# A bidirectional state-space layer's scan chains joined in pairs, its phasor tables packed, and new instruction durations in the list scheduler

## The chip, the cores and the metric

The kernel runs on one core of a Trainium2 chip. The metric is the device time of one execution in microseconds. The profile comes from one execution that the hardware profiler recorded. TensorE (PE) multiplies matrices, VectorE (DVE), ScalarE (ACT) and GpSimd (POOL) work on elements, and SyncE (SP) issues the transfers.

## What is computed

One layer of a hybrid encoder over 2048 positions and 1024 channels. A modulated RMS norm and one input projection feed three groups of heads; their outputs are joined, projected, normed and added to the input; a gated MLP with a depthwise convolution of width 3 follows.

```python
h = rms_norm(x, g_pre_mix[l]) * (1.0 + sc_m) + sh_m
u, f, q, k, v = jnp.split(h @ w_in[l], splits, axis=-1)
y_ssm = s5_mixer(u, ...)         # 24 groups x 16 channels, 64 complex states, two directions
y_fft = fourier_mixer(f, w_fft[l])       # 2-D DFT over positions and channels
y_att = window_attention(q, k, v, sink[l])       # +-128 positions, 6 query heads
y = concatenate([y_ssm, y_fft, y_att]) @ w_out[l]
x = x + gt_m * rms_norm(y, g_post_mix[l])
# then: norm, w_up, convolution, gelu(gate) * val, w_down, norm, gated residual add
```

The part that matters here is `s5_mixer`: for each group and each direction a linear recurrence h[t] = a h[t-1] + b u[t] with a complex diagonal a runs along the positions (backwards for the second direction), and y is read from both directions' states.

## The kernel before

**How the recurrence is tiled.** Eight positions are folded into one step, so that a group's input `U` is a 128x256 tile (8 positions x 16 channels, by 256 steps). A group has 64 states, each with a real and an imaginary part, so its states fill 128 partitions; two directions of 256 steps make a row of 512. VectorE's scan instruction knows no complex numbers. The kernel therefore turns the states by a phase so that each scan has a real factor: a row of 256 steps is split into 16 blocks of 16, table `t1c`/`t1s` holds the cosine and sine of the phase at each place of a block, and `t2c`/`t2s` those at the 16 block ends. The tables are tiles of 16x48: place first, then the 48 pairs of group and direction.

**One chain** (`s5_chain`, L953 on) handles one group. TensorE makes the two projections XA and XB in PSUM. VectorE multiplies each by a table (`gg`, `tt_`), adds them, and scans 512 elements. The block ends (2 directions x 16) then go through nine small instructions of 32 or 30 elements, with two products by a permutation matrix on TensorE between them (it swaps real and imaginary halves), and one of the nine is a scan over the 16 block ends. The result is added to the first place of each block, the 512 elements are scanned again, and two more products by `t1s` and `t1c` lead to the closing matrix products, a copy and a store. The two calls that read the tables are

```python
tsel = lambda tab: tab[:, :, s0:s0 + 2].rearrange("p b d -> p d b")
ta = yield from self.tt(ta, v4(gg), v4(XA), bt(tsel(self.t1c)), M)
```

so that the table's innermost step is 48 elements (L968, L980).

**Pairs.** `s5_pair` (L861 on) prepares two groups at once: projection matrices on POOL (on VectorE for the first two pairs), transposed by TensorE; output matrices on POOL; a small matrix `M0` by eight transfers. It puts two entries in a queue, one for each group. Three workers (`N_CH`) take entries from it. There are 12 pairs, 24 groups, and room for three pairs in preparation.

**What sets the order.** The whole kernel is written as processes that yield the engine, a duration and the time from which their inputs are there. A list scheduler (`Sched.run`) always emits the instruction that can start earliest by these numbers, and among equals the one of the higher rank; each engine then runs its instructions in the emitted order. Chains rank before the input projections, Fourier heads and output parts, which fill the gaps. Durations stand in the helpers: `tt` (L275, a tensor_tensor), `ts` (L280, a tensor_scalar), `scan` (L300). Every matmul is issued at L318, every activation at L272, every transfer at L267. PSUM is shared by tags: four banks `s` for the chains and, later, attention; three `z`; one `m`.

**What follows.** The gated unit of the state-space heads, the attention (16 blocks of 128 positions, two workers), Fourier products and the rest of the input projection share the time after the scans; then come the output projection, the norms and the MLP.

Of the kernel before, what the change touches and what calls it, by code (L numbers as in the profile page):

```python
# [16 lines left out]
P = 128  # L17
# [26 lines left out]
S5_MUL = "V"  # L44
# [29 lines left out]
N_CH = 3  # L74
# [128 lines left out]
class Builder:  # L203
# [71 lines left out]
    def tt(self, t, out, a, b, op, eng="V"):  # L275
        t = yield (eng, 0.07 + (0.00105 if eng == "V" else 0.0022) * cols(out), t)
        (self.V if eng == "V" else self.G).tensor_tensor(out, a, b, op)  # L277
# [22 lines left out]
    def scan(self, t, out, d0, d1):  # L300
        t = yield ("V", 0.1 + 0.00105 * cols(out), t)
        self.V.tensor_tensor_scan(out, d0, d1, 0.0, ALU.mult, ALU.add)  # L302
        return t + self.LAT
# [114 lines left out]
    def setup(self):  # L418
# [8 lines left out]
        self.par, self.sgn = self.const([P, 3, 48]), self.const([P, 1])  # L427
# [302 lines left out]
    def s5_consts(self):  # L730
# [98 lines left out]
        for f in ends:  # L829
            t = max(t, (yield ("w", f)))  # L830
# [4 lines left out]
        self.t1c, self.t1s, self.t2c, self.t2s = tabs  # L835
# [25 lines left out]
    def s5_pair(self, b, t, slots):  # L861
# [44 lines left out]
        left = [2, 0.0]  # L906
# [46 lines left out]
    def s5_chain(self):  # L953
        PE = self.PE
        v4 = lambda a: a.rearrange("p (d a b) -> p d a b", d=2, a=16)
        v3 = lambda a: a.rearrange("p (d a) -> p d a", d=2)
        fl = lambda a: a.rearrange("p d a -> p (d a)")
        bt = lambda a: a.unsqueeze(2).to_broadcast([P, 2, 16, 16])
        M, ADD, SUB = ALU.mult, ALU.add, ALU.subtract
        while True:  # L960
            while not self.s5q:
                if self.s5n == 0:
                    return
                yield ("w", self.f_s5q)
            b, g, t, f_u, f_m, wt, U, RT, M0, Vf, Vs, left, slots = self.s5q.pop(0)
            t = max(t, (yield ("w", f_u)))
            s0 = 4 * b + 2 * g
            tsel = lambda tab: tab[:, :, s0:s0 + 2].rearrange("p b d -> p d b")  # L968
            tb_ = yield ("acq", self.bank["s"], 2)
            XA, XB = self.ps("s"), self.ps("s")  # L970
            rhs = (U[:, g, :], U[:, g, ::-1])
            ops = [(XX[:, d * 256:d * 256 + 256], wt[:, 2 * g + d, o:o + 128], rhs[d], True, True)
                   for XX, o in ((XA, 0), (XB, 64)) for d in range(2)]
            ta = yield from self.mm(max(t, tb_), ops[:2])
            tb = yield from self.mm(max(t, tb_), ops[2:])
            t12, rxs = self.u([2, 512]), self.u([768])
            gg, tt_ = t12[:, 0], t12[:, 1]
            rx, sc = rxs[:, 0:512], self.shape(rxs[:, 512:768], [8, 2, 16])
            tx = yield from self.act(t, v4(rx), bt(RT[:, 0, 2 * g:2 * g + 2]), AF.Copy)
            ta = yield from self.tt(ta, v4(gg), v4(XA), bt(tsel(self.t1c)), M)  # L980
            tb = yield from self.tt(tb, v4(tt_), v4(XB), bt(tsel(self.t1s)), M)
            self.free(tb, XB)
            t = yield from self.tt(max(ta, tb), gg, gg, tt_, ADD, eng=S5_ADD)
            t = yield from self.scan(max(t, tx), tt_, rx, gg)

            pe_ = XA
            ends = v4(tt_)[:, :, :, 15]
            c2, s2 = tsel(self.t2c), tsel(self.t2s)
            tc_ = yield from self.tt(t, sc[:, 1], ends, c2, M)
            t = yield from self.mm(t, [(pe_[:, 0:32], self.perm, ends, True, True)])  # L990
            t = yield from self.tt(t, sc[:, 0], v3(pe_[:, 0:32]), s2, M)
            t = yield from self.tt(t, sc[:, 1], sc[:, 1], sc[:, 0], ADD)
            t = yield from self.scan(t, fl(sc[:, 2]), fl(RT[:, 1, 2 * g:2 * g + 2]), fl(sc[:, 1]))
# [1120 lines left out]
```

## Time and profile before

| | us |
|---|---|
| median of three runs | 2199.02 (2198.71 to 2199.77) |
| the profiled execution's own time | 2203.73 |
| its span, first to last instruction | 2202.0 |
| TensorE busy | 2004.0 (91%) |
| VectorE busy | 1597.4 (73%) |
| ScalarE busy | 984.3 (45%) |
| POOL busy | 246.6 (11%) |
| mean granted TensorE clock | 0.955 of full speed |

A row of groups reads: line of the program, engine, operation, output <- inputs with shapes (u is a tile in SBUF, ps one in PSUM, c a constant, d a tensor in memory), number of instructions, then busy time in us and mean ns of one, then the engine's idle time just before them and what ended most of it. A row of stretches gives the stretch and its length, each engine's busy time with its instructions, the granted TensorE clock, the share of the transfer engines and GB/s. A row of waits gives who waited for whom, us in total, times and the longest. A row of the timeline gives the start, the length, the engine, the line and the instruction. A float32 matmul leaves two records.

### The profile page before, as it was taken

How to read it: one execution, taken by the hardware profiler on the slowest of the kernel's cores; microseconds unless marked ns; L12 is line 12 of the kernel's file. 1: busy time of each engine (PE TensorE's matmuls, PEld its weight loads, DVE VectorE, ACT ScalarE, POOL GpSimd, SP SyncE). 2: the span in 40 equal slices, each digit the busy share in tenths (PEclk: the TensorE clock that was granted, in tenths of full speed). 3: DMA queues.
4: the chain of work that ended last, by engine and by line, in shares of the span. 5: the costliest groups of instructions: out<-in, count | busy, mean ns of one | idle time of the engine just before them, and what ended most of it. 6: DMA issues, size and time to landing. Idle time of an engine off the chain costs nothing.

```text
span 2202.0 us, 27575 instructions
## 1 busy us (share of the span) xinstructions
PE 2004.0 (91%) x10120; PEld 1001.0 (45%) x10120; DVE 1597.4 (73%) x2400; ACT 984.3 (45%) x1670; POOL 246.6 (11%) x310
## 2 busy tenths in 40 slices
PE   6778787889998858898999999999999999999997
PEld 2335565445454425443444444444444444444445
DVE  8999999886676584879988885565656665446456
ACT  3623233336576556556655553444444433222321
POOL 0565545020100000000000000000000000011002
PEclk9988898999999979799999999999999999999998
DMA  9351123673735273335655557565656494538533
GB/s 367 105 190 60 41 93 135 210 267 124 241 118 173 95 244 103 114 127 210 244 205 186 187 187 300 195 220 203 219 201 224 144 343 143 182 119 292 188 110 110
DMA packets 206667, 397.31 MB, mean 180 GB/s; under 512 B 19522, under 2 KB 111939, under 8 KB 206531
## 3 DMA queue, kind: packets, MB, share of 16 engines
q1 hardware_dynamic: 206530, 395.55, 52.2%
q8 instruction: 79, 1.29, 0.2%
q14 instruction: 58, 0.47, 0.1%
HBM read 258.93 MB, written 134.98 MB: 179 GB/s over the span
## 4 chain that ended last, share of the span: by engine, by line
PE 61%; DVE 25%; ACT 5%; issue 4%; DMA 3%; POOL 1%; SPq 1%; DVEq 0%; POOLq 0%; ACTq 0%
PE ps L318 61%; DVE u L277 12%; DVE u L291 8%; ACT u L272 5%; DVE u L302 2%; DVE u L446 1%; DMA u<-d 1%; POOL u L277 1%; SPq L267 1%; DMA u<-w_up 1%; DMA d<-u 1%; DVE u L284 0%; DVE u L410 0%; DMA u<-x 0%; DVE u L1327 0%
## 5 line engine op out<-in xcount | busy, mean ns | idle before, releaser
L318 PE MATMUL ps<-u,u 128*128 128x512 f16 (+9 forms) x9306 | 1918.7, 366 | 123.5 <-DVE u L277 35.7
L318 PEld LDWEIGHTS <-u 128*128 128x128 f16 (+1 forms) x9334 | 872.2, 101 | 1041.1 <-issue 174.5
L277 DVE TENSOR_TENSOR u<-u,u 128x512 f32<-128x512 f32 (+10 forms) x596 | 512.0, 892 | 107.0 <-ACT u L272 90.0
L272 ACT ACTIVATE u<-u 128x1024 f16<-128x1024 f32 (+8 forms) x483 | 403.2, 868 | 364.3 <-DVE u L277 158.8
L272 ACT ACTIVATE u<-ps 128x512 f32<-128x512 f32 (+6 forms) x511 | 276.3, 556 | 471.3 <-PE ps L318 445.7
L291 DVE SCALAR_TENSOR_TENSOR u<-u,c,u 128x1023 f32<-128x1023 f32 (+5 forms) x248 | 291.0, 1197 | 60.9 <-ACT u L272 55.2
L291 DVE SCALAR_TENSOR_TENSOR u<-ps,u 128x512 f32<-128x512 f32 (+3 forms) x231 | 152.4, 666 | 242.7 <-PE ps L318 201.1
L291 DVE SCALAR_TENSOR_TENSOR u<-u,u 128x1024 f16<-128x1024 f32 (+7 forms) x225 | 240.8, 1093 | 59.2 <-ACT u L272 55.8
L277 POOL TENSOR_TENSOR u<-u,u 128x288 f32<-128x288 f32 (+9 forms) x169 | 188.2, 1129 | 628.2 <-DVE u L291 459.1
L272 ACT ACTIVATE u<-u,c 128x1023 f32<-128x1023 f32 (+2 forms) x104 | 120.1, 1158 | 142.1 <-DVE u L291 122.0
L307 POOL MEMSET u<- 128x1 f32 x88 | 8.7, 99 | 1139.4 <-PE ps L318 510.9
L272 ACT ACTIVATE u<-u,st 128x384 f32<-128x384 f32 (+3 forms) x192 | 108.8, 596 | 35.6 <-DVE st L284 20.1
L318 PEld LDWEIGHTS ps<-u,u 128*128 128x128 f32 (+1 forms) x532 | 95.9, 194 | 62.3 <-DVE u L277 33.9
L277 DVE TENSOR_TENSOR u<-u 128x512 f32<-128x512 f32 (+8 forms) x184 | 92.3, 513 | 23.6 <-ACT u L272 22.4
L318 PE MATMUL ps<-u,c 128*128 128x32 f32 (+4 forms) x190 | 67.9, 465 | 43.7 <-DVE u L302 19.3
L318 PE MATMUL ps<-c,u 128*128 128x128 f16 (+1 forms) x568 | 61.9, 231 | 17.9 <-ACT u L272 11.4
L272 ACT ACTIVATE c<-u 128x2 f32<-128x2 f32 (+1 forms) x88 | 17.9, 203 | 130.3 <-DVE u L291 130.1
L1327 DVE CUSTOM_DVE_ANT_0 u<-ps,u 128x384 f32<-128x384 f32 (+1 forms) x96 | 49.1, 537 | 30.0 <-PE ps L318 29.3
L302 DVE TENSOR_TENSOR_SCAN u<-u,u 128x512 f32<-128x512 f32 (+1 forms) x72 | 68.9, 964 | 1.1 <-ACT u L272 0.9
L318 PEld LDWEIGHTS ps<-u,c 128*128 128x128 f32 (+1 forms) x190 | 30.7, 185 | 77.2 <-DVE u L302 29.7
L291 DVE SCALAR_TENSOR_TENSOR u<-u,st,u 128x384 f16<-128x384 f32 (+1 forms) x96 | 55.7, 609 | 11.9 <-ACT u L272 11.6
L277 DVE TENSOR_TENSOR u<-ps,u 128x512 f32<-128x512 f32 (+2 forms) x96 | 56.0, 600 | 7.6 <-PE ps L318 6.9
(52 smaller groups left out, 367.2 us busy)
## 6 DMA issues: line engine op xcount, KB each, us to landing
u<-d SPq DMA_DIRECT2D x226, 512.0 KB
d<-u SPq DMA_DIRECT2D x158, 512.0 KB
d<-u SPq DMA_DIRECT2D x111, 256.0 KB
u<-w_ada SPq DMA_DIRECT2D x48, 512.0 KB
u<-w_up SPq DMA_DIRECT2D x44, 512.0 KB
u<-d SPq DMA_DIRECT2D x66, 256.0 KB
u<-x SPq DMA_DIRECT2D x32, 512.0 KB
u<-d SPq DMA_DIRECT2D x24, 511.0 KB
```

The costliest lines, as they stand in the source:

```text
L267: self.SP.dma_start(out, in_)
L272: self.S.activation(out, in_, func, **kw)
L277: (self.V if eng == "V" else self.G).tensor_tensor(out, a, b, op)
L291: self.V.scalar_tensor_tensor(out, a, s, b, op0, op1)
L302: self.V.tensor_tensor_scan(out, d0, d1, 0.0, ALU.mult, ALU.add)
L307: (self.V if eng == "V" else self.G).memset(out, v)
L318: self.PE.matmul(o, a, b, start=st, stop=sp, skip_group_check=chain)
L446: V.tensor_tensor_reduce(out=w, in0=w, in1=self.crep, op0=ALU.mult, op1=ALU.add, scale=1.0, scalar=0.0, accum_out=mod[:, j:j + 1])
L1327: V.tensor_tensor_reduce(out=s_, in0=o, in1=self.bias[h // 2][:, h % 2, bo:bo + nk * 128], op0=ALU.add, op1=ALU.max, scale=1.0, scalar=-3e ...
```

## The change

1. The four tables are copied by ScalarE into tiles of 48x16 (the pair of group and direction first, the place innermost). The sign that VectorE put on the two sine tables is now a scale of the copy, from a new constant `nsg`.
2. One queue entry is a pair. A worker makes the opening part for both groups in turn (two PSUM banks each, freed after the products), then the small part once for both (60 or 64 elements), then the closing part for each. One further bank holds the block ends' products and both groups' results.
3. Two workers take the entries.
4. The durations of `tt` on both engines, `ts` on POOL and `scan` change.

```diff
-N_CH = 3
+N_CH = 2
...
     def tt(self, t, out, a, b, op, eng="V"):
-        t = yield (eng, 0.07 + (0.00105 if eng == "V" else 0.0022) * cols(out), t)
+        t = yield (eng, 0.155 + 0.00104 * cols(out) if eng == "V" else 0.4 + 0.0024 * cols(out), t)
...
     def ts(self, t, out, a, s1, s2, op0, op1=None, eng="V"):
-        t = yield (eng, 0.12 + (0.0008 if eng == "V" else 0.001) * cols(out), t)
+        t = yield (eng, 0.15 + (0.0008 if eng == "V" else 0.0018) * cols(out), t)
...
     def scan(self, t, out, d0, d1):
-        t = yield ("V", 0.1 + 0.00105 * cols(out), t)
+        t = yield ("V", 0.08 + 0.0023 * cols(out), t)
...
-        for ts_ in (t1s, t2s):
-            t = yield from self.ts(t, ts_, ts_, self.sgn, -1.0, M, M)
+        tn = yield from self.ts(0, self.nsg, self.sgn, -1.0, None, M)
+        byst = []
+        for f, (x, y) in zip(ends, ((t1c, t1s), (t2c, t2s))):
+            tf = yield ("w", f)
+            for src, sc in ((x, 1.0), (y, self.nsg)):
+                dst = self.u([48, 16])
+                t1 = yield from self.act(max(tf, tn), dst, src.rearrange("p j s -> p s j"), AF.Copy, scale=sc)
+                t = max(t, t1)
+                byst.append(dst)
...
-        for g in range(2):
-            self.s5q.append((b, g, max(tp, tr), f_u, f_m, wt, U, RT, M0, Vf, Vs, left, slots))
-            f, self.f_s5q = self.f_s5q, Fut()
-            f.set(0)
+        self.s5q.append((b, max(tp, tr), f_u, f_m, wt, U, RT, M0, Vf, Vs, slots))
+        f, self.f_s5q = self.f_s5q, Fut()
+        f.set(0)
...
+            gg, tt_, rx = (self.u([2, 512]) for _ in range(3))
+            sc = self.u([7, 4, 16])
+            tc, ts_, c2, s2 = (tab[:, 4 * b:4 * b + 4] for tab in (self.t1c, self.t1s, self.t2c, self.t2s))
+            for g in range(2):
+                ds = slice(2 * g, 2 * g + 2)
+                tb_ = yield ("acq", self.bank["s"], 2)
+                XA, XB = self.ps("s"), self.ps("s")
...
+                ta = yield from self.tt(ta, v4(gg[:, g]), v4(XA), bt(tc[:, ds]), M)
+                tb = yield from self.tt(tb, v4(tt_[:, g]), v4(XB), bt(ts_[:, ds]), M)
+                self.free(ta, XA)
+                self.free(tb, XB)
+                t = yield from self.tt(max(ta, tb), gg[:, g], gg[:, g], tt_[:, g], ADD, eng=S5_ADD)
+                t = yield from self.scan(max(t, tx), tt_[:, g], rx[:, g], gg[:, g])
+            tb_ = yield ("acq", self.bank["s"], 1)
+            pe_ = self.ps("s")
...
-            t = yield from self.mm(t, [(pe_[:, 0:32], self.perm, ends, True, True)])
+            t = yield from self.mm(t, [(pe_[:, 0:64], self.perm, ends, True, True)])
...
+            for g in range(2):
+                ds = slice(2 * g, 2 * g + 2)
+                t = yield from self.scan(tk, tt_[:, g], rx[:, g], gg[:, g])
+                t1 = yield from self.tt(t, v4(rx[:, g]), v4(tt_[:, g]), bt(ts_[:, ds]), M, eng=S5_MUL)
+                t = yield from self.tt(t, v4(gg[:, g]), v4(tt_[:, g]), bt(tc[:, ds]), M)
...
+                y = pe_[:, 256 * g:256 * g + 256]
```

The order in which the built programs' instructions stand shows the move. A scan is the row SCALAR_TENSOR_TENSOR of L302 there. VectorE before, in the small part of two chains that stand beside each other (u_1407 and u_1408 belong to one group, u_1448 and u_1449 to another; u_89 and u_90 are the tables of the block ends):

```order
L277 TENSOR_TENSOR u_1449<-u_1448,u_89 128x32
L307 MEMSET u_1370 128x8
L905 COPY u_1370<-c_82 128x4x15 x2
L277 TENSOR_TENSOR u_1372<-u_1372,ps_1506 16x2x16
L277 TENSOR_TENSOR u_1372<-u_1372 16x2x16
L277 TENSOR_TENSOR u_1408<-ps_1387,u_90 128x2x15
L277 TENSOR_TENSOR u_1449<-ps_1422,u_90 128x32
L277 TENSOR_TENSOR u_1408<-u_1408 128x2x15
L277 TENSOR_TENSOR u_1449<-u_1449 128x32
L277 TENSOR_TENSOR u_1408<-u_1408,c_82 128x2x15
```

VectorE now, at a like place (u_1376 and u_1379 belong to one pair, u_1265 to u_1267 to another; u_1063 and u_1078 are the packed tables of the places, u_1098 and u_1108 those of the block ends):

```order
L302 SCALAR_TENSOR_TENSOR u_1379<-u_1132,u_1379 128x64
L277 TENSOR_TENSOR u_1134<-u_1134,ps_1522 16x2x16
L277 TENSOR_TENSOR u_1379<-u_1379,u_1098 128x4x15
L277 TENSOR_TENSOR u_1134<-u_1134 16x2x16
L277 TENSOR_TENSOR u_1379<-ps_1487,u_1108 128x4x15
L277 TENSOR_TENSOR u_1267<-u_1266,u_1078 128x512
L277 TENSOR_TENSOR u_1379<-u_1379 128x4x15
L277 TENSOR_TENSOR u_1265<-u_1266,u_1063 128x512
L277 TENSOR_TENSOR u_1379<-u_1379,c_82 128x4x15
```

The small steps are twice as wide and come once for a pair, and a 512-wide product of the other pair stands between them where small steps of other groups stood.

TensorE before, late in the scans (c_79 is the permutation, ps_2820 a tile of the rest of the projections, u_2621 to u_2623 a pair's opening products):

```order
L318 MATMUL ps_2820<-u_194,u_590 128x512
L318 MATMUL ps_2638<-u_2657,c_79 128x32
L318 LDWEIGHTS u_590
L318 MATMUL ps_2820<-u_196,u_590 128x512
L318 MATMUL ps_2843<-u_2621,u_2623 128x256
L896 MATMUL ps_2764<-c_78,u_2671 128x128 x4
L318 MATMUL ps_2843<-u_2621,u_2623 128x256
L318 MATMUL ps_2844<-u_2621,u_2623 128x256 x2
```

TensorE now, a little past the middle of the scans (ps_2357 holds a closing pair's results, ps_2519 a tile of the projections):

```order
L318 MATMUL ps_2519<-u_659,u_1164 128x512
L318 MATMUL ps_2357<-u_2002,u_2003 128x256
L318 MATMUL ps_2357<-u_2255,u_2003 128x255 x2
L318 MATMUL ps_2357<-u_2257,u_2002 128x255 x2
L318 MATMUL ps_2496<-u_2408,c_79 128x64
L318 MATMUL ps_2551<-u_2272,u_84 16x128 x4
L318 LDWEIGHTS u_1164
L318 MATMUL ps_2519<-u_657,u_1164 128x512
```

A permutation now serves four rows of block ends, and tiles of 24 projection matmuls stand around the chains' steps from the middle of the scans on; ahead of the last permutation there stand 736 matmuls of 128x512, 476 before. From matmul 4103 before and 4112 now (of 9751 and 9727) TensorE's order is the same for 4452 matmuls.

More of the change, by code (lines that the diff above doesn't have):

```diff
@@ L964, in s5_chain @@
                 yield ("w", self.f_s5q)
[L965 to L973, printed above, removed]
@@ L982, in s5_chain @@
[L982 to L988, printed above, removed]
+            b, t, f_u, f_m, wt, U, RT, M0, Vf, Vs, slots = self.s5q.pop(0)
+            t0 = max(t, (yield ("w", f_u)))
+            gg, tt_, rx = (self.u([2, 512]) for _ in range(3))
+            sc = self.u([7, 4, 16])
@@ L997, in s5_chain @@
[L997 removed]
+            t = yield from self.mm(t, [(pe_[:, 64:128], self.perm, fl(sc[:, 2]), True, True)])
+            t = yield from self.tt(t, sc[:, 3, :, 1:16], v3(pe_[:, 64:128])[:, :, 0:15], s2[:, :, 1:16], M)
             t = yield from self.tt(t, k1, k1, sc[:, 3, :, 1:16], SUB)
[L999 to L1000 removed]
@@ L1013, in s5_chain @@
-            t = yield from self.mm(max(t, tm), ops)
-            t = yield from self.act(t, U[:, g], y, AF.Copy)
-            self.free(t, XA)
-            r = slice(16 * (2 * b + g), 16 * (2 * b + g) + 16)
-            t = yield from self.dma(t, self.yd[r].rearrange("c t k -> t c k"), U[:, g])
-            left[0] -= 1
-            left[1] = max(left[1], t)
-            if left[0] == 0:
-                slots.give(left[1])
-                self.f_yd[b].set(left[1])
+            t = yield from self.tt(t, k1, k1, self.rho[:, 0, 4 * b:4 * b + 4].unsqueeze(2).to_broadcast([P, 4, 15]), M)
@@ new lines, in s5_chain @@
+            first = gg.rearrange("p g (d a b) -> p (g d) a b", d=2, a=16)[:, :, 1:16, 0]
+            tk = yield from self.tt(t, first, first, k1, ADD)
+            tm = yield ("w", f_m)
+            for g in range(2):
[3 more added lines that the diff above has]
+                t = yield from self.tt(t, v4(gg[:, g]), v4(tt_[:, g]), bt(tc[:, ds]), M)
+                t = max(t, t1)
+                y = pe_[:, 256 * g:256 * g + 256]
+                ops = [(y, M0[:, g, :], U[:, g, :], True, False)]
+                for j, pp in ((0, gg[:, g]), (1, rx[:, g])):
+                    ops.append((y[:, 1:256], Vf[:, 2 * g, 16:144] if j == 0 else Vs[:, 2 * g], pp[:, 0:255], False, False))
+                    ops.append((y[:, 0:255], Vf[:, 2 * g + 1, 0:128] if j == 0 else Vs[:, 2 * g + 1],
+                                pp[:, 256:511][:, ::-1], False, j == 1))
+                t = yield from self.mm(max(t, tm), ops)
+                t = yield from self.act(t, U[:, g], y, AF.Copy)
+                r = slice(16 * (2 * b + g), 16 * (2 * b + g) + 16)
+                fs.append((yield from self.dma(t, self.yd[r].rearrange("c t k -> t c k"), U[:, g])))
@@ L1025, in f_evac @@
+            self.free(t, pe_)
+            slots.give(max(fs))
+            self.f_yd[b].set(max(fs))
     def f_evac(self, t, ps, dst, done):
```

48 lines of the change are left out of this document (15 added, 33 removed).

## The prediction

> **What bounds the kernel now.** I read the page first, then the busy time of each engine by stage, then the instruction groups and the waits of the one stage that the change rewrites. The page's slices:
>
> ```profile
> PE   6778787889998858898999999999999999999997
> DVE  8999999886676584879988885565656665446456
> PEclk9988898999999979799999999999999999999998
> ```
>
> TensorE is busy throughout, except in the first eight slices (some 440 us), where VectorE stands at 8 to 9 tenths and TensorE at 6 to 8, at a lower clock. I cut the span where the scans begin and end (161.5 to 423 us) and where the page changes character:
>
> ```profile
> core 0: us, PE busy (x) PEld busy (x) DVE busy (x) ACT busy (x) POOL busy (x), PEclk, DMA share, GB/s
> 0.00:161.50 161.50, 121.60 (x441) 49.30 (x442) 147.23 (x300) 72.42 (x99) 71.30 (x63) 0.90 0.64 226
> 161.50:423.00 261.50, 207.06 (x1168) 149.87 (x1167) 251.09 (x482) 82.27 (x172) 117.41 (x120) 0.90 0.29 93
> 423.00:500.00 77.00, 70.07 (x392) 34.64 (x390) 60.60 (x85) 29.41 (x44) 16.49 (x15) 0.98 0.83 275
> 500.00:650.00 150.00, 146.13 (x998) 78.78 (x997) 102.39 (x272) 89.45 (x222) 6.69 (x5) 0.99 0.51 169
> 650.00:740.00 90.00, 78.19 (x494) 41.79 (x495) 53.80 (x116) 55.39 (x114) 0.00 (x0) 0.94 0.49 144
> 740.00:875.00 135.00, 104.00 (x631) 55.89 (x628) 87.77 (x180) 77.68 (x155) 0.00 (x0) 0.87 0.45 150
> 875.00:1130.00 255.00, 230.36 (x1064) 106.50 (x1064) 223.51 (x248) 156.20 (x231) 2.18 (x22) 0.93 0.48 176
> 1130.00:1970.00 840.00, 835.27 (x3856) 378.00 (x3856) 541.99 (x570) 359.51 (x541) 12.56 (x70) 1.00 0.58 202
> ```
>
> In the scan stage VectorE is 96% busy (251.1 of 261.5) and TensorE idles 261.5 - 207.1 = 54.4 us: the stage is VectorE's. After it TensorE is the scarce engine. From 423 to 875 us it idles 452 - (70.07 + 146.13 + 78.19 + 104.00) = 53.6 us, and from 1130 on hardly at all. So the end moves by what TensorE's idle and busy time loses up to the place from which its order is the same (matmul 4103). The rows hold 441 + 1168 + 392 + 998 + 494 + 631 = 4124 records up to 875 us; some 340 are second records of float32 matmuls, so the place lies 319 matmuls on, at 1064/255 = 4.2 a microsecond near 950 us. Microseconds of VectorE count only as far as TensorE stops waiting for them.
>
> **The change part by part.** VectorE's groups in the scan stage:
>
> ```profile
> L302 DVE TENSOR_TENSOR_SCAN u<-u,u 128x512 f32<-128x512 f32 x48 | 61.7, 1286 | 1.1 <-ACT u L272 0.9
> L277 DVE TENSOR_TENSOR u<-u,u 128x512 f32<-128x512 f32 x47 | 52.2, 1147 | 0.1
> L277 DVE TENSOR_TENSOR u<-ps,u 128x512 f32<-128x512 f32 x46 | 46.0, 1010 | 1.4 <-PE ps L318 0.9 <-DMA d<-u 0.4
> L277 DVE TENSOR_TENSOR u<-u 128x512 f32<-128x512 f32 x23 | 18.1, 792 | 0.1
> L277 DVE TENSOR_TENSOR u<-u,u 128x30 f32<-128x30 f32 x48 | 14.9, 314 | 0.2
> L277 DVE TENSOR_TENSOR u<-u,u 128x32 f32<-128x32 f32 x24 | 8.0, 334 | 0.1
> L277 DVE TENSOR_TENSOR u<-u 128x32 f32<-128x32 f32 x24 | 7.7, 321 | 0.0
> L302 DVE TENSOR_TENSOR_SCAN u<-u,u 128x32 f32<-128x32 f32 x24 | 7.7, 320 | 0.0
> L277 DVE TENSOR_TENSOR u<-u 128x30 f32<-128x30 f32 x24 | 7.4, 310 | 0.1
> L277 DVE TENSOR_TENSOR u<-u,c 128x30 f32<-128x30 f32 x24 | 7.0, 297 | 0.1
> L277 DVE TENSOR_TENSOR u<-ps,u 128x32 f32<-128x32 f32 x24 | 4.5, 189 | 1.9 <-PE ps L318 1.8
> L277 DVE TENSOR_TENSOR u<-ps,u 128x30 f32<-128x30 f32 x24 | 4.5, 189 | 3.6 <-PE ps L318 3.5
> L291 DVE SCALAR_TENSOR_TENSOR u<-ps,u 128x512 f16<-128x512 f32 x6 | 4.1, 678 | 0.0
> ```
>
> *The tables.* Of the 512-wide products, 48 read a phasor table and PSUM (1010 ns) and 48 a table and SBUF (1147 ns); three fall outside the window. The add of the same width, both inputs in SBUF and no table, takes 792 ns; a 512-wide instruction that reads PSUM without a table takes 678 ns. These means hold whatever POOL does beside them. Near the stage's end POOL is quiet, and the gap is there too:
>
> ```profile
> 411.72 1.91 DVE L277 TENSOR_TENSOR u<-ps,u 128x512 f32<-128x512 f32 x2
> 414.03 0.67 DVE L277 TENSOR_TENSOR u<-u 128x512 f32<-128x512 f32 x1
> 417.17 0.19 DVE L277 TENSOR_TENSOR u<-u 128x32 f32<-128x32 f32 x1
> 421.67 1.23 DVE L302 TENSOR_TENSOR_SCAN u<-u,u 128x512 f32<-128x512 f32 x1
> 422.93 1.97 DVE L277 TENSOR_TENSOR u<-u,u 128x512 f32<-128x512 f32 x2
> ```
>
> A table product takes 0.95 to 0.99 us against 0.67 for the add, so I put the gap down to the table's inner step of 48 elements. Packed, I take the plain instruction's price: 48 x (1.147 - 0.792) = 17.0 us and 48 x (1.010 - 0.678) = 15.9 us saved, 32.9 together. The bounds are 32.9 and nothing, if something else in these products is slow. [...]
>
> *The packing itself* is four copies of 768 elements on ScalarE, where VectorE no longer scales two tables. The nearest row, from the first 200 us:
>
> ```profile
> L272 ACT ACTIVATE u<-u 128x1024 f32<-128x1024 f32 x16 | 15.9, 1046 | 6.5 <-DMA u<-x 6.5
> ```
>
> At most 4 x 1.05 = 4.2 us (the strided reads could cost more, up to twice as an estimate from the products above), beside a ScalarE that is busy 72.4 of 161.5 us there. I price it at nothing, because VectorE works on the first pairs' projection matrices meanwhile; without that cover the first products start up to 4.2 us later, and that much is in the range.
>
> *The small steps.* The eight groups of 30 and 32 elements sum to 14.9 + 8.0 + 7.7 + 7.7 + 7.4 + 7.0 + 4.5 + 4.5 = 61.7 us for 216 instructions. Half of them go. The 108 that stay are 32 elements wider, at (0.67 - 0.19)/480 = 1.0 ns an element: 108 x 0.032 = 3.5 us. Saved: 30.9 - 3.5 = 27.4 us. The 48 long scans stay as they are.
>
> *VectorE's sum.* 251.1 - 32.9 - 27.4 = 190.8 us. In the order of the changed program some 25 other instructions now stand inside the stage: 13 more of the 678 ns kind (8.8 us), eight folds of 1023 or 1024 elements (some 1.2 us each, as an estimate by the 1.0 ns an element, 9.8 us), a few more: some 20 us. So 211 us in place of 251.
>
> *TensorE's sum.* The order counts 476 of the 128x512 matmuls ahead of the last permutation before and 736 now: 260 matmuls of projections and Fourier products move ahead of the stage's end. The rows for them and for the permutations, then TensorE's waits in the stage (us in total, times, longest), and last the price of a 512-wide matmul between 1200 and 1700 us:
>
> ```profile
> L318 PE MATMUL ps<-u,u 128*128 128x512 f16 x141 | 35.8, 388 | 0.3 <-ACT u L272 0.3
> L318 PE MATMUL ps<-u,c 128*128 128x32 f32 x96 | 18.8, 288 | 19.5 <-DVE u L302 19.3
> ```
>
> ```profile
> PE ps L318 <- DVE u L277: 24.4, 18, 3.0
> PE ps L318 <- DVE u L302: 19.3, 20, 2.8
> ```
>
> ```profile
> L318 PE MATMUL ps<-u,u 128*128 128x512 f16 x2319 | 500.7, 379 | 0.0
> ```
>
> In this stage they cost 35.8/141 = 0.254 us each, 66.0 us; later they would have cost 500.7/2319 = 0.216, 56 us. Half of the permutations go: -9.4 us. TensorE's stage comes to 207.1 + 66.0 - 9.4 = 263.7 us, over VectorE's 211. So TensorE becomes the bound, and I expect the scans to end where they end now, give or take 20 us, with 56 us of later work already done. The gain is the idle time that vanishes. Of the 54.4 us, the two rows of waits give 43.7 to VectorE. There are half as many permutations to wait for and twice as much filler between them; I take 20 us for what is left (the bounds are about 8, the pairs' start alone, and 54, nothing gained). That is -34.4 - 9.4 = -43.8 us.
>
> *423 to 875 us.* Here TensorE has 56 us less to do, and its waits are of other kinds:
>
> ```profile
> PE ps L318 <- ACT u L272: 19.3, 13, 5.1
> PE ps L318 <- DMA u<-d: 12.0, 3, 7.1
> ```
>
> These are latencies of the attention blocks, which less filler covers less well. But the order also leaves 150 more of the 512-wide matmuls behind the start of the fourteenth attention block (1496 stand ahead of it, 1646 before), which is where the idle 31.0 us of 740 to 875 lie. I take +5 us, with -15 and +45 as bounds.
>
> *The new durations* are only numbers in the list scheduler; they cost no instruction. On TensorE the order after about 950 us is the same apart from a few rows of the tail, so I price that part at 0. VectorE's is not the same up to about 1130 us, and TensorE idles 24.6 us from 875 to 1130; I take 0 there, within 5 either way.
>
> *Two workers for three.* Each now carries a pair. A worker holds two banks in its opening part and one afterwards, so the four banks carry both workers. I price it at 0; the slow rival prices it otherwise.
>
> *Sum.* The profiled execution took 2203.7 us (span 2202.0). 2203.7 - 34.4 - 9.4 + 5 = 2164.9. It lies 4.7 us over the median of the runs, 2199.0, so the forecast for the median is **2160 us**.
>
> **The rivals.**
> *A larger gain.* TensorE idles only 8 us in the stage (-46.4 and -9.4), and the matmuls left behind the fourteenth block fill half of the 31.0 us: -15.5. That is -71, 2128 us. For it: the moved matmuls outlast VectorE's work by 53 us. Against it: an order made from fixed durations slips where POOL slows VectorE.
> *Given back later.* The stage gains 43.8, but the attention blocks run at their own latency, and TensorE idles 36 us more from 423 to 875: -8, 2191 us. For it: ScalarE and DMA lead the waits there. Against it: VectorE and ScalarE are busy only 304.6 and 251.9 of 452 us.
> *Packing gains nothing.* The products stay at 1.0 to 1.15 us. VectorE needs 244 of TensorE's 263.7 us, slips more often, and 35 us of idle stay: -28.8 + 5, about 2175 us. The row at 0.67 us speaks against it. [...]
> *Slower: matmul runs ahead of the chain.* A pair passes TensorE five times in a row (two openings, two permutations, the closing products), and TensorE takes its queue in order. If each passage waits behind a tile of 24 matmuls, 24 x 0.254 = 6.1 us, a pair needs its own 22 us (opening 2 x (0.68 + 0.68 + 0.67 + 1.23) = 6.5, nine small steps at some 0.22 and two permutations at the longest wait of 2.8 = 7.6, closing 2 x (1.23 + 0.67 + 0.67) = 5.1, last products some 3 as an estimate) and 30.5 more: 53. Six rounds of two workers give 318 us for 261.5, which eats the 56 us of moved work, and 20 us more are missing as filler later: 2220 us. It decides once a pair takes over 263.7/6 = 44 us. For it: the order shows such runs. Against it: in the stage TensorE waited for VectorE, hardly the reverse (0.9, 1.8 and 3.5 us in the rows above). That the new durations do nothing is excluded by the order.
>
> **How the numbers follow.** I give the forecast 0.48, the larger gain 0.15, packing without gain 0.10, given back 0.15, slower 0.12. About 0.2% (4.4 us) is what a measurement here can tell from no change. Of "given back", with 8 us, 0.06 falls within that and 0.09 stays faster. So faster 0.48 + 0.15 + 0.10 + 0.09 = 0.82, same 0.06, slower 0.12. The range runs from the larger gain, 2128, to just past "given back" and an unmoved time, 2200; it leaves out the slow rival and the tail below.
>
> **What would show it.** Right: table products at 0.7 to 0.8 us; 108 small instructions of 60 and 64 elements near 0.35; TensorE idle 20 us from the first to the last scan; the last scan at 400 to 445 us; a similar idle up to the second half. Wrong: products still at 1.0; VectorE waiting for TensorE by tens of microseconds in the stage; the last scan past 460 us; or an idle time between there and 875 us that has grown by as much as the scan stage lost.

## The result, and the profile after

Four runs of the changed kernel gave a median of 2178.77 us (2175.01 to 2182.36), four of the kernel before on the same chip 2198.86 (2197.23 to 2199.77). The ratio is 0.991, with a 95% interval from 0.989 to 0.993: 20 us faster, about half of the 39 us that were forecast. The profiled execution took 2179.9 us, with a span of 2178.1. Its slices on TensorE and VectorE:

```profile
PE   6879987978998749997999999999999999999997
...
DVE  8897787877775583889988884666666655457356
...
PEclk9999998999999859998999999999999999999998
```

TensorE now has 7 to 9 tenths from the second slice on, so the scan stage is fuller. In its place there is a dip to 4, at a clock of 5 tenths, in the fifteenth slice (762 to 817 us). The stages of the changed kernel, cut at its own first and last scan and at 926 us. That last cut lies some 12 us ahead of the matmul from which TensorE's order is that of before (matmul 4112), and in the kernel before the cut at 949 us lies some 11 us ahead of it (matmul 4103 there):

```profile
core 0: us, PE busy (x) PEld busy (x) DVE busy (x) ACT busy (x) POOL busy (x), PEclk, DMA share, GB/s
0.00:172.50 172.50, 130.09 (x574) 58.17 (x575) 151.58 (x304) 83.28 (x114) 76.80 (x74) 0.93 0.62 221
172.50:442.00 269.50, 231.25 (x1366) 157.65 (x1364) 221.00 (x394) 90.06 (x187) 118.48 (x113) 0.95 0.38 121
442.00:740.00 298.00, 265.28 (x1666) 143.89 (x1667) 206.44 (x484) 186.25 (x385) 17.41 (x16) 0.95 0.54 175
740.00:800.00 60.00, 24.14 (x116) 12.37 (x114) 50.34 (x79) 39.59 (x71) 0.00 (x0) 0.58 0.46 157
800.00:926.00 126.00, 115.64 (x679) 61.76 (x680) 79.30 (x130) 73.19 (x140) 0.20 (x2) 0.93 0.38 125
926.00:2178.00 1252.00, 1211.30 (x5676) 557.65 (x5674) 841.84 (x905) 531.68 (x794) 34.07 (x106) 0.99 0.57 199
```

The stretch of the kernel before that answers to the third to fifth row:

```profile
423.00:949.00 526.00, 458.93 (x2813) 242.50 (x2812) 365.27 (x722) 300.16 (x612) 23.38 (x22) 0.93 0.51 168
```

The way to this cut became 23 us shorter (22 to the common matmul itself). The first scan comes 11.0 us later (172.5 for 161.5), the stage is 8.0 us longer (269.5 for 261.5), and the stretch behind it is 42 us shorter (484 for 526). TensorE idles 269.5 - 231.3 = 38.3 us in the stage, 54.4 before; and 484 - 405.1 = 78.9 us behind it, 67.1 before. Over the span its idle time did not fall (2178.1 - 1977.7 = 200.4, before 2202.0 - 2004.0 = 198.0). All of the gain stands in its busy time, 26 us less. Some 8 us of that are the permutations, of which half as many stand in the stage (18.8 us in the prediction's row):

```profile
L318 PE MATMUL ps<-u,c 128*128 128x64 f32 x48 | 10.5, 310 | 20.5 <-DVE u L302 20.5
```

VectorE's groups in the changed kernel's stage:

```profile
L302 DVE TENSOR_TENSOR_SCAN u<-u,u 128x512 f32<-128x512 f32 x48 | 61.4, 1293 | 0.5
L277 DVE TENSOR_TENSOR u<-u,u 128x512 f32<-128x512 f32 x68 | 48.9, 736 | 0.4
L277 DVE TENSOR_TENSOR u<-ps,u 128x512 f32<-128x512 f32 x46 | 30.0, 677 | 21.2 <-PE ps L318 16.7 <-DMA u<-u 4.5
L291 DVE SCALAR_TENSOR_TENSOR u<-u,u 128x1024 f16<-128x1024 f32 x14 | 17.2, 1227 | 18.9 <-ACT u L272 18.9
...
L277 DVE TENSOR_TENSOR u<-u,u 128x60 f32<-128x60 f32 x24 | 7.7, 321 | 0.4
...
L302 DVE TENSOR_TENSOR_SCAN u<-u,u 128x64 f32<-128x64 f32 x12 | 5.7, 475 | 0.1
L277 DVE TENSOR_TENSOR u<-u,u 128x64 f32<-128x64 f32 x12 | 5.0, 415 | 0.0
```

The products cost 0.74 and 0.68 us, 1.15 and 1.01 before (the row of 68 holds the 48 products and some 20 adds, whose two inputs now lie in different tiles). But VectorE has an idle time that it did not have: 269.5 - 221.0 = 48.5 us (10.4 before), ahead of the products that read PSUM and ahead of the folds (the 1024-wide steps of L291, which prepare inputs for TensorE's other matmuls). The waits of VectorE in the stage say for whom:

```profile
DVE u L291 <- ACT u L272: 21.5, 7, 7.3
DVE u L277 <- PE ps L318: 17.4, 10, 5.3
```

The waits of TensorE in the stage:

```profile
PE ps L318 <- DVE u L302: 20.5, 14, 5.6
PE ps L318 <- DVE u L291: 7.6, 3, 4.6
```

VectorE waits for ScalarE and for TensorE, and TensorE waits for VectorE: no engine sets the stage alone. And the start, in TensorE's timeline:

```profile
160.97 5.32 PE L318 MATMUL ps<-u,u 128*128 128x128 f16 x51 [8.32 <-DVE u L291]
166.12 0.61 PE L901 MATMUL ps<-c,u 128*128 128x128 f32 x4
166.56 3.29 PE L318 MATMUL ps<-u,u 128*128 128x128 f16 x32
169.69 0.60 PE L901 MATMUL ps<-c,u 128*128 128x128 f32 x4
```

The first transposes of the state-space stage (L901) stand behind 51 filler matmuls (matmuls of other parts that the scheduler puts into gaps), which themselves waited 8.3 us for a fold. They start at 166.1 us, 154.3 before. That is where the 11 us are.

### The profile page after: what moved, and what is told of

It reads as the page before. It is cut to its first block, busy times and chain, and to the rows that moved or that the text cites. A ratio compares the mean times of both kernels' runs of the same rounds, so it can differ in the third digit from the quotient of the medians.

```text
span 2178.1 us, 27424 instructions
## 1 busy us (share of the span) xinstructions
PE 1977.7 (91%) x10072; PEld 991.5 (46%) x10072; DVE 1550.5 (71%) x2291; ACT 1004.0 (46%) x1686; POOL 247.0 (11%) x310
## 4 chain that ended last, share of the span: by engine, by line
PE 63%; DVE 22%; ACT 6%; DMA 4%; issue 4%; SPq 1%; POOL 0%; DVEq 0%; POOLq 0%; ACTq 0%
PE ps L318 63%; DVE u L277 10%; DVE u L291 8%; ACT u L272 5%; DVE u L302 2%; SPq L267 1%; DMA u<-w_out 1%; DMA u<-d 1%; DMA u<-w_up 1%; ACT L272 1%; DVE u L446 1%; DVE u L1332 0%; DVE u L410 0%; DVE u L284 0%; DMA u<-w_in 0%
## 5 line engine op out<-in xcount | busy, mean ns | idle before, releaser
L318 PE MATMUL ps<-u,u 128*128 128x512 f16 (+10 forms) x9306 | 1886.7, 363 | 109.7 <-DVE u L291 45.9
L272 ACT ACTIVATE u<-u 128x1024 f16<-128x1024 f32 (+7 forms) x485 | 405.2, 869 | 377.8 <-DVE u L277 151.8
L277 DVE TENSOR_TENSOR u<-u,u 128x512 f32<-128x512 f32 (+11 forms) x584 | 500.3, 888 | 103.0 <-ACT u L272 91.0
L272 ACT ACTIVATE u<-ps 128x512 f32<-128x512 f32 (+5 forms) x511 | 275.5, 555 | 443.6 <-PE ps L318 405.7
L291 DVE SCALAR_TENSOR_TENSOR u<-u,c,u 128x1023 f32<-128x1023 f32 (+5 forms) x248 | 288.8, 1183 | 70.7 <-ACT u L272 53.7
L291 DVE SCALAR_TENSOR_TENSOR u<-ps,u 128x512 f32<-128x512 f32 (+3 forms) x231 | 152.1, 664 | 229.2 <-PE ps L318 190.3
L291 DVE SCALAR_TENSOR_TENSOR u<-u,u 128x1024 f16<-128x1024 f32 (+7 forms) x225 | 239.7, 1088 | 73.6 <-ACT u L272 70.5
L272 ACT ACTIVATE u<-u,c 128x1023 f32<-128x1023 f32 (+3 forms) x106 | 123.2, 1165 | 129.3 <-DVE u L291 104.9
L318 PEld LDWEIGHTS ps<-u,u 128*128 128x128 f32 (+1 forms) x532 | 90.1, 177 | 33.1 <-DVE u L277 10.6
L318 PE MATMUL ps<-u,c 128*128 128x512 f32 (+4 forms) x142 | 60.2, 538 | 45.9 <-DVE u L302 20.5
L277 DVE TENSOR_TENSOR u<-u 128x512 f32<-128x512 f32 (+8 forms) x136 | 69.7, 520 | 18.1 <-ACT u L272 17.1
L302 DVE TENSOR_TENSOR_SCAN u<-u,u 128x512 f32<-128x512 f32 (+1 forms) x60 | 67.1, 1130 | 0.6
L291 DVE SCALAR_TENSOR_TENSOR u<-u,st,u 128x384 f16<-128x384 f32 (+1 forms) x96 | 55.6, 606 | 11.0 <-ACT u L272 10.8
L272 ACT ACTIVATE u<-u,c,c 128x512 f32<-128x512 f32 (+1 forms) x64 | 49.3, 804 | 24.0 <-DVE u L277 9.9
L284 DVE TENSOR_SCALAR u<-ps 128x512 f16<-128x512 f32 x48 | 32.9, 686 | 37.3 <-PE ps L318 33.3
```

The costliest lines, as they stand in the source:

```text
L272: self.S.activation(out, in_, func, **kw)
L284: e.tensor_scalar(out, a, s1, s2, op0)
L291: self.V.scalar_tensor_tensor(out, a, s, b, op0, op1)
L318: self.PE.matmul(o, a, b, start=st, stop=sp, skip_group_check=chain)
```

## The experiments

The change is three things at once: packed tables, joined pairs on two workers, new durations. The prediction's theory (A) is that VectorE's work in the scan stage sets the time, so the packing and the joining bring the gain and the durations are only numbers. The first rival (B) is that the order, thus the durations, bring it.

**Packing alone**, and joining and durations alone, all against the kernel before:

```diff
 packing alone: kernel before, with
+ dst = self.u([48, 16]) ... self.act(..., dst, src.rearrange("p j s -> p s j"), AF.Copy, scale=sc)
- tsel = lambda tab: tab[:, :, s0:s0 + 2].rearrange("p b d -> p d b")
+ tsel = lambda tab: tab[:, s0:s0 + 2]
 joining alone: the changed kernel, with tables and durations as before
 durations alone: kernel before, with the new lines of tt, ts and scan
 joining and packing: the changed kernel, with
-        t = yield ("V", 0.08 + 0.0023 * cols(out), t)
+        t = yield ("V", 0.1 + 0.00105 * cols(out), t)
 and tt and ts likewise as before
```

> The kernel before with the packed tables alone (single groups, three workers, old durations). If VectorE's work in the scan stage decides (theory A): 96 products fall from about 1.08 to about 0.75 us, VectorE loses some 30 us there, and since it was 96% busy the time falls by 20 to 30 us, to about 2172. If the order of the instructions decides (theory B, the new durations bring the gain), the order hardly changes here and the time stays within 6 us of 2199.

> The changed kernel with strided tables and the old durations: only the joining of the two groups and the two workers. Theory A: 108 fewer small instructions, 27 us less for VectorE in the stage, time 15 to 25 us under 2199. Theory B: within 6 us of 2199, or slower, because the scheduler still takes the scans for half as long as they are.

> The kernel before with the new durations alone. Theory A: VectorE's work is the same and still bounds the scan stage, so at most 10 us under 2199, though more projection matmuls may move into the stage. Theory B: most of the 20 us are here, 2180 or less.

> The changed kernel with the old durations: packed and joined. Theory A: VectorE has some 60 us less in the scan stage, so 30 to 45 us under 2199 unless TensorE takes over as the bound, in which case like the changed kernel, 2179. Theory B: near 2199, because the new durations are missing.

The first four rows stand against 15 runs of before with a median of 2200.12 us, the last against the four of the first section; the later kernels have runs of before of their own (medians 2197.56 and 2199.30 us), so kernels are compared by their ratios. The last column is the start of the last 512-wide scan.

| kernel | median us | ratio to before, 95% interval | last scan at us |
|---|---|---|---|
| packing alone | 2167.99 | 0.985 (0.984 to 0.987) | 386.3 |
| joining alone | 2195.85 | 0.998 (0.997 to 0.999) | 446.3 |
| durations alone | 2217.95 | 1.008 (1.007 to 1.009) | 467.1 |
| joining and packing | 2168.49 | 0.986 (0.985 to 0.987) | 421.3 |
| all three (the change) | 2178.77 | 0.991 (0.989 to 0.993) | 440.5 |

Packing alone is faster than the whole change. TensorE's order is in it instruction for instruction that of before, so this is theory A at its cleanest, and its gain is a little over the 20 to 30 us that A forecast. Stage and two groups of packing alone (the prediction's rows of before: 261.5 us, VectorE 251.09, TensorE 207.06 with 1168 records, clock 0.90):

```profile
161.00:387.50 226.50, 188.75 (x1168) 137.25 (x1166) 219.38 (x480) 80.96 (x170) 121.20 (x117) 0.97 0.34 108
```

```profile
L277 DVE TENSOR_TENSOR u<-u,u 128x512 f32<-128x512 f32 x46 | 37.5, 850 | 0.1
L277 DVE TENSOR_TENSOR u<-ps,u 128x512 f32<-128x512 f32 x45 | 29.8, 675 | 0.2
```

VectorE saved 31.7 us and the stage became 35 us shorter. The products that read SBUF stay at 0.85 us here, above the 0.74 of the changed kernel's row and the prediction's 0.79. The same holds in the joined order, where the two kernels, joining alone and joining with packing, have TensorE's order in common too:

```profile
161.00:447.50 286.50, 224.10 (x1286) 154.57 (x1285) 261.13 (x403) 92.84 (x187) 130.28 (x124) 0.90 0.36 116
```

```profile
161.00:422.50 261.50, 214.31 (x1289) 149.92 (x1288) 232.18 (x403) 90.70 (x184) 122.76 (x121) 0.93 0.40 127
```

VectorE saved 28.9 us, the stage 25.0 and the run 27. On joining, theory A missed: with strided tables it brought 4 us, which is theory B's figure. On packed ones the 32 us under before lie at the edge of A's 30 to 45, but packing alone has them too, so joining brought nothing there (the two intervals overlap nearly wholly), though VectorE has some 27 us less of small steps. The second row shows where they went: VectorE idles 261.5 - 232.2 = 29.3 us, in packing alone 226.5 - 219.4 = 7.1. On the durations both theories missed: they cost 18 us alone and 10 on the joined and packed kernel.

**Do the durations cost the same on packed tables?** The rival here is that they mattered only beside the strided ones.

```diff
 packing alone, with
-        t = yield ("V", 0.1 + 0.00105 * cols(out), t)
+        t = yield ("V", 0.08 + 0.0023 * cols(out), t)
 and tt and ts likewise new
```

> The kernel before with the packed tables and the new durations (single groups, three workers). Theory D (the new durations cost the time, whatever else is in the kernel): packing alone came to 2168 us, the durations alone cost 18 us on the kernel before and 10 us on the changed one, so 2178 to 2186, with the first scan at about 173 instead of 161 us. Rival R (the durations hurt only beside the strided tables, whose products they underestimate): within 3 us of packing alone, 2165 to 2171. Converse rival J (the joined group is what the durations suit): over 2186.

2168.8 us, 0.988 (0.986 to 0.989), the rival's figure: at most a few us more than packing alone. Yet the first scan comes at 173.4 us and the last at 439.7, 53 us later than in packing alone. So a late scan stage is no loss by itself: 699 of the 512-wide matmuls stand ahead of its last permutation, 476 in packing alone, and that work is missing behind it.

**Is it the start or what follows?** The durations were switched at the point where the constants of the state-space stage are done:

```diff
 new durations only late (and the converse, only early):
-        t = yield ("V", 0.08 + 0.0023 * cols(out), t)
+        t = yield ("V", ((0.08 + 0.0023 * cols(out)) if self.f_s5c.done else (0.1 + 0.00105 * cols(out))), t)
 and tt and ts likewise
```

> The changed kernel, with the old durations until the constants of the state-space stage are done and the new ones from then on. Its TensorE order has 344 matmuls of 512 columns ahead of the first transposes, as with the old durations, and 702 ahead of the last permutation (736 in the changed kernel, 623 with the old durations throughout). Theory S (most of the durations' loss is the first scan 11 to 12 us later, because more filler stands ahead of the first transposes): first scan at 161 to 162 us, time 2166 to 2171. Rival L (the loss is in the scan stage and the attention behind it, where still more filler is moved ahead): 2176 to 2183 though the first scan is early.

> The converse: the new durations until the constants of the state-space stage are done, the old ones from then on. 395 matmuls of 512 columns ahead of the first transposes, 659 ahead of the last permutation. Theory S (the late start is the loss): first scan at 172 to 173 us, 2176 to 2182. Rival L (the loss comes later): 2166 to 2171 in spite of the late first scan.

Only late: 2164.84 us (2159.34 to 2172.69), 0.986 (0.984 to 0.988), first scan at 160.9, the time a little under the 2166 to 2171 of the theory of the late start. Only early: 2173.46, 0.990 (0.988 to 0.991), first scan at 172.5. The late half costs nothing that can be told, as that theory has it. The early half's time lies between the two forecasts, some 8 us over the old durations' by the ratios. That would support the late start, were it not that the kernel above starts as late and loses next to nothing.

**Is it what stands behind the scans?** Here the new durations hold until the last state-space result is out, and the old ones from there:

```diff
-        t = yield ("V", 0.08 + 0.0023 * cols(out), t)
+        t = yield ("V", ((0.08 + 0.0023 * cols(out)) if not all(f.done for f in self.f_yd) else (0.1 + 0.00105 * cols(out))), t)
 and tt and ts likewise
```

> The changed kernel with the new durations until the last state-space result is out, and the old ones from there on. Up to there its order is that of the changed kernel (first transposes behind 395 matmuls of 512 columns, last permutation behind 736), so first and last scan should stay at 172 and 439 us. Theory B2 (what the new durations cost lies behind the scan stage, where they reorder the attention's work and TensorE waits 52.6 us for ScalarE between 442 and 926 us, against 23.8 with the old durations): 2163 to 2170, and that wait falls to 24 to 36 us. Rival F (it lies in the filler that the stage has used up, so that the work behind it stands uncovered whatever the durations are there): 2175 to 2182, wait above 45 us.

2169.55 us, 0.987 (0.985 to 0.988), below the change's interval. First and last scan stay at 173.0 and 439.6 us, within 1 us of the changed kernel. TensorE's wait for ScalarE between 440 and 950 us, first in the changed kernel:

```profile
PE ps L318 <- ACT u L272: 52.6, 27, 14.8
```

and with the old durations behind the scans:

```profile
PE ps L318 <- ACT u L272: 29.6, 26, 3.8
```

So in the changed kernel the 9 to 10 us that the durations cost lie behind the scans, in the order of the attention's work there. Its longest, in the changed kernel's timeline, is the end of the page's dip (740 to 800 us, 24.14 us busy of 60, at a clock of 0.58):

```profile
805.94 1.80 PE L318 MATMUL ps<-c,u 128*128 128x128 f16 x12 [14.84 <-ACT u L272]
```

It cannot be put on the durations' values, though. The same row with new durations only late, the kernel at 0.986 (this profiled execution took 2172.7 us, the longest of its five):

```profile
PE ps L318 <- ACT u L272: 43.1, 26, 14.6
```

and with packing and new durations throughout, at 0.988:

```profile
PE ps L318 <- ACT u L272: 57.3, 17, 12.0
```

Both wait nearly as long or longer, and by their medians lose next to nothing. What is lost depends on which order comes out as a whole.

**Are two workers too few for joined pairs?**

```diff
 joining and packing, old durations
-N_CH = 2
+N_CH = 3
```

> Joined groups and packed tables with the old durations, and three workers instead of two. With two workers this was 2168.5 us, no faster than packing alone (2168.0), although VectorE had some 27 us less to do: in the scan stage VectorE then stood idle for 29 us, against 7 us with packing alone. Theory W (two workers of joined groups are too few to cover the chain's latency, so the saved work turns into idle time): VectorE's idle time in the stage falls to 5 to 12 us, the last scan comes 15 to 20 us earlier (at about 402 to 406 instead of 421 us), and the time falls to 2150 to 2162. Rival T (in that stage TensorE's and ScalarE's filler, not the chain, has become the bound): 2165 to 2171, last scan at 415 us or later, or the filler that was moved out comes back as idle time of TensorE behind the stage.

2192.7 us, 0.998 (0.997 to 0.999). The last scan does come early, at 396.0 us, 25 us before that of two workers, and VectorE idles 16.7 us in place of 29.3 (5 to 12 were forecast):

```profile
161.00:397.20 236.20, 197.53 (x1201) 140.60 (x1200) 219.46 (x383) 84.81 (x175) 133.04 (x120) 0.96 0.34 109
```

But the run is 24 us longer. Only 539 of the 512-wide matmuls now stand ahead of the last permutation (623 with two workers), and what is behind has to run them and waits more. At the 0.248 us each that the account below uses, those 84 matmuls are 21 of the 25 us. The theory was right that the scans end earlier, but most of that is filler moved out, and it was wrong on the time; the rival's second clause, that the gain comes back behind the stage, holds, and by far more than it allowed.

**Does VectorE still set the stage once the tables are packed?** The order was kept and four of the nine small steps of each group left out, so the kernel no longer computes the layer:

```diff
 packing alone, with
-            (self.V if eng == "V" else self.G).tensor_tensor(out, a, b, op)
+            if emit:
+                (self.V if eng == "V" else self.G).tensor_tensor(out, a, b, op)
 and emit=False for the four steps
```

> The kernel before with packed tables, and four of the nine small steps of each of the 24 groups left out (those that work in place: the two that combine the products, the one by the decay, the one that puts the carries into the stage's input), so the output is not the state-space result; the planner still counts them, so TensorE's order stays (476 matmuls of 512 columns ahead of the last permutation, 767 ahead of the first attention block). That takes 96 instructions of about 0.21 us, some 20 us, off VectorE in the scan stage, nearly what joining the groups saves (27 us). Theory A (at the order of before VectorE still sets the stage, and joining's saving was lost only through the order that comes with it): 20 us off packing alone, 2145 to 2151, last scan at about 366 us. Rival T (with packed tables TensorE and the latency of the chain already set the stage): 2160 to 2168, VectorE's idle time in the stage grows by 12 us or more.

2164.26 us, 0.984 (0.983 to 0.985): 4 us at most, the rival's figure. VectorE's idle time in the stage grows by 9.4 us (7.1 to 16.6), less than the rival's 12. (Up to some local exchanges the order on TensorE is that of before.) Two small steps and VectorE's wait for TensorE in packing alone (161 to 387.5 us):

```profile
L277 DVE TENSOR_TENSOR u<-u,u 128x32 f32<-128x32 f32 x24 | 6.8, 284 | 0.1
...
L302 DVE TENSOR_TENSOR_SCAN u<-u,u 128x32 f32<-128x32 f32 x24 | 5.7, 237 | 0.0
```

```profile
DVE u L277 <- PE ps L318: 4.1, 4, 2.1
```

and without the four steps (its lines are one higher):

```profile
L303 DVE TENSOR_TENSOR_SCAN u<-u,u 128x32 f32<-128x32 f32 x24 | 10.3, 433 | 0.1
...
L278 DVE TENSOR_TENSOR u<-u,u 128x32 f32<-128x32 f32 x24 | 8.3, 346 | 0.0
```

```profile
DVE u L278 <- PE ps L319: 13.8, 6, 5.7
```

```profile
161.00:385.30 224.30, 185.34 (x1164) 138.44 (x1163) 207.74 (x385) 80.98 (x170) 128.79 (x118) 0.96 0.34 109
```

VectorE's busy time in the stage falls by 219.4 - 207.7 = 11.6 us only, since the steps that stay become longer (the small scan 237 to 433 ns). And 9.7 of those 11.6 us turn into waits for TensorE. The last scan comes 2 us earlier. That is what the joining ran into: with packed tables, VectorE's small steps are hardly what the stage waits for any more.

**How much does an order move the time when nothing is meant by it?** One constant, the time between a result and its use, was raised by 0.01 us:

```diff
 packing alone; then joining and packing
-    LAT = 0.12
+    LAT = 0.13
```

> A control: packing alone with the planner's constant for the time between a result and its use raised from 0.12 to 0.13 us, nothing else; 474 matmuls of 512 columns ahead of the last permutation (476), 1598 ahead of the fourteenth attention block (1633). If small shifts of the order move the time little: 2165 to 2171. Theory N (the order behind the scan stage moves the time by 5 to 20 us whatever the numbers mean): outside 2162 to 2174.

> The same control on joined groups with packed tables and the old durations (2168.5 us): 0.13 instead of 0.12. Here the order moves more: 566 matmuls of 512 columns ahead of the last permutation instead of 623, 758 ahead of the first attention block instead of 729. If the time between last scan and the common point only trades filler for filler at 0.22 us each, the last scan comes 12 us earlier (at about 409 us) and the time stays within 4 us, 2164 to 2173. Theory N: outside 2162 to 2175, with the difference in TensorE's waits for ScalarE behind 440 us.

Packing alone: 2162.22 us, 0.983 (0.981 to 0.984), 6 us less by the ratios. Joining and packing: 2204.2 us, 1.003 (1.001 to 1.004), 36 us more. The first lies at the edge between its two forecasts. In the second the filler-for-filler theory missed, and the other, that the order behind the scans moves the time whatever the numbers mean, holds: a trifle in one constant moves this kernel by as much as any part of the change. TensorE's waits from 440 to 950 us in the slow one:

```profile
PE ps L318 <- ACT u L272: 42.1, 28, 14.2
PE ps L318 <- DMA u<-d: 17.4, 3, 16.7
```

and the two long ones in its timeline:

```profile
806.09 2.08 PE L318 MATMUL ps<-u,u 128*128 128x384 f16 x6 [16.72 <-DMA u<-d]
831.99 1.81 PE L318 MATMUL ps<-c,u 128*128 128x128 f16 x12 [14.23 <-ACT u L272]
```

The same kernel with 0.12 has, for the first row:

```profile
PE ps L318 <- ACT u L272: 23.8, 18, 9.0
```

The waits are less than half of the 36 us, though. Over the span TensorE's idle time grew by 14.5 us (2201.7 - 1985.7 = 216.0 for 2166.2 - 1964.7 = 201.5), as other waits became shorter; its busy time for the same number of records grew by 21.

**One account for all.** Stage and rest can be told apart if the filler that was moved is put back at a price: the changed kernel's stage has 348 of the 512-wide matmuls:

```profile
L318 PE MATMUL ps<-u,u 128*128 128x512 f16 x348 | 86.4, 396 | 4.9 <-DVE u L291 4.6 <-ACT u L272 0.3
```

86.4/348 = 0.248 us each. The column "stage" is the start of the last 512-wide scan less 0.248 us for each of these matmuls ahead of the last permutation beyond 476; "rest" is the span behind it, with that filler added, against packing alone. It is an estimate, since other work moved as well: a price lower by 0.05 us would move 13 us from "rest" to "stage" in the rows with 736. And the spans are those of the profiled executions, which lie 8 us over their kernel's median for "only late", 4 over it for "old behind the scans" and for before, and 4 under it for joining alone.

| kernel | matmuls ahead | last scan us | stage us | rest us |
|---|---|---|---|---|
| before | 476 | 421.7 | 422 | 0 |
| packing alone | 476 | 386.3 | 386 | 0 |
| the same, four steps left out | 476 | 384.1 | 384 | -2 |
| the same, 0.13 | 474 | 391.0 | 392 | -12 |
| packing and durations | 699 | 439.7 | 384 | +3 |
| joining alone | 623 | 446.3 | 410 | 0 |
| joining and packing | 623 | 421.3 | 385 | +1 |
| the same, 0.13 | 566 | 407.4 | 385 | +37 |
| the same, three workers | 539 | 396.0 | 380 | +29 |
| durations alone | 663 | 467.1 | 421 | +16 |
| the change, durations new only late | 702 | 435.4 | 379 | +12 |
| the change, durations new only early | 659 | 416.4 | 371 | +20 |
| the change, old behind the scans | 736 | 439.6 | 375 | +17 |
| the change | 736 | 440.5 | 376 | +22 |

Each kernel with packed tables has its stage at 371 to 392, each with strided ones at 410 to 422. At one order the packing moves the stage by 35 us (single groups) and 25 (joined); the 21 us between the packed kernels are largely within what the price of the filler leaves open. The rest spreads over some 50 us, and no part of the change orders it.

The best version here is packing alone with 0.13, faster than both kernels. Nothing was meant by its 6 us over packing alone; they are what this order happened to give.

## Why the prediction was half right

*The tables* were worth what was forecast: products at 0.74 and 0.68 us, VectorE's busy time 31.7 us less and 32 us of time where TensorE's order stays the same (32.9 were forecast). The traces show that the step of 48 elements cost time: a product that reads PSUM took 1.01 us strided before and 0.68 packed, in the changed kernel and in packing alone. No other step was tried, and why this one costs was not shown. The rival by which packing gains nothing is out, and that its 2175 us lies nearest to the measured time is a coincidence.

*The packing's price* was too low in size, right in effect. The copies, on ScalarE in the changed kernel:

```profile
L272 ACT ACTIVATE u<-u,c 128x768 f32<-128x768 f32 x2 | 3.3, 1630 | 8.9 <-POOL u L277 8.9
L272 ACT ACTIVATE u<-u 128x768 f32<-128x768 f32 x2 | 3.1, 1530 | 0.0
```

That is 6.4 us, not 4.2, yet hidden as forecast: with packing alone the first scan comes at 160.9 us (161.5 before).

*The small steps* cost what was forecast, but the time they saved was worth next to nothing (4 us at most where four of them were left out). The step that let TensorE become the bound took it that work taken from VectorE would come back as filled TensorE time. In the run with four steps left out it came back as waits of VectorE for TensorE.

*TensorE's sum*, 263.7 us, failed: it was 231.3. For one part it put all 260 moved matmuls into the stage. The stage has 348 of them for 141, 207 more, since 51 went ahead of the first transposes: some 53 x 0.254 = 13 us too much. For the other part it took TensorE's busy time of before as work. It is not: with the same 1168 records in the same order it went from 207.1 to 188.8 us when only VectorE became faster, and the clock from 0.90 to 0.97. In the changed kernel the stage's other matmuls show the same: 231.3 - 86.4 - 10.5 = 134.4 us, 207.1 - 35.8 - 18.8 = 152.5 before. Those 18 us and the 13 are the gap. So TensorE did not become the bound. The idle time of the stage that was to fall from 54 to 20 us fell to 38, and over the span it did not fall at all (200 us, 198 before). The gain came as 26 us less busy time, of which the forecast held only the 9.4 of the permutations. That the time fell at all is no luck, as the products became cheaper as forecast; that it fell inside the range is in part.

*The sum* itself had a gap. 260 matmuls that cost 66 us in the stage and 56 later are a loss of 10 us, and the sum left it out. With it the forecast would have been 2170 us. Joining and packing without the new durations took 2168.5, but that agreement is luck too: TensorE idles 261.5 - 214.3 = 47.2 us in its stage, not 20.

*The new durations*, "only numbers", were priced at 0, within 5 us. They cost 10 us on the joined and packed kernel, as much as the gap in the sum, 18 on the kernel before, and at most a few on packing alone. The bound was wrong more than the value: an order that comes out of a list scheduler was shown to move the time by 6 us down and 36 up at a change of 0.01 us in one constant.

*Behind the scans*: +5 us was forecast for 423 to 875 us; up to the cut ahead of the common matmul TensorE's idle time grew by 78.9 - 67.1 = 11.8 us. The rival "given back later" was right in kind, but had 36 us; its 2191 us did not come true. The later start of the scans, 11 us, was no term of the sum at all.

*Two workers* were priced at 0: in the joined and packed kernel three let the scans end 25 us earlier, and the run becomes 24 us longer. *The slow rival* named a pair at over 44 us as its point; at 269.5/6 = 44.9 us the stage stood there, with 17.4 us of waits of VectorE for TensorE, but the table above puts the change's loss behind the scans.

What stays open: which property of an order makes the work behind the scans wait. The waits were shown; why one order has them and the next one not was not settled.

## What to carry to other kernels

Make a change that leaves the order alone first, and measure it by itself: the packed operand gave 32 us, one for one with the engine that set the stage, and more than the whole change. Where a scheduler lays the order, price a change of its numbers not at nothing but by a control, one constant moved by a trifle, before a difference of 10 us is put down to anything. And do not add up a stage from the busy time of an engine that idles there.

## What the runs showed of the hardware

A 512-wide float32 product on VectorE took 0.30 to 0.41 us more where one input stepped by 48 elements (1.01 us before against 0.68 packed where it read PSUM, 1.15 against 0.74 to 0.85 where it read SBUF; the 0.74 is the mean of a row of the changed kernel that holds some adds too). A copy of 768 such elements on ScalarE took 1.53 to 1.63 us in the changed kernel.

TensorE's busy time was not a constant of its work: in the scan stage the same records in the same order took 207.1 us before, at a granted clock of 0.90, where it idled 54.4 us, and 188.8 in packing alone, at 0.97, where it idled 37.7. In the changed kernel's dip from 740 to 800 us, where it was busy for 24.14 of 60 us, the clock was 0.58, and from 926 us on, where it was busy for 1211.30 of 1252, it was 0.99. What makes the clock fall was not tried.

The time that the traces show for a short step on VectorE was not the step's alone: with the in-place add ahead of the small scan left out, and three more in-place steps, the scan took 433 ns in place of 237. Why was not tried.
